# Buffer addresses in a two-layer decoder trunk: a large set that steps by 4096 bytes, and three single tiles

## The chip, the cores and the metric

The kernel runs on one core of one Trainium2 chip. The metric is the device time of one launch in microseconds; the time before is 2398.49 us, the median of three runs (2398.19 to 2398.84). A profile of one execution is there beside the times.

## The reference

A trunk of two layers over 1024 tokens of width 1024, in float32. Layer 0 mixes by an mLSTM with eight heads (key width 64, value width 128) in chunks of 128 tokens. Layer 1 mixes by causal latent attention with eight heads. Each layer ends in an MLP of hidden width 4096 with a squared ReLU, and each norm is modulated by columns computed from the condition `c`.

```python
for l in range(DEPTH):
    sh1, sc1, g1, sh2, sc2, g2 = jnp.split(cond @ ada_w[l] + ada_b[l], 6, axis=-1)
    h = modulate(rmsnorm(x, norm_g[l, 0]), sh1, sc1)
    y = mlstm_mixer(h, ...) if l < N_A else mla_mixer(h, ..., k_nope, k_rope, v, cos, sin)
    x = x + g1[:, None, :] * rmsnorm(y, norm_g[l, 1])
    h = modulate(rmsnorm(x, norm_g[l, 2]), sh2, sc2)
    y = jnp.square(jax.nn.relu(h @ mlp_w1[l])) @ mlp_w2[l]
    x = x + g2[:, None, :] * rmsnorm(y, norm_g[l, 3])
```

In the mLSTM, per chunk: `C_new = decay * C + sum_s w_s k_s v_s^T`, and the output is the sum of a part inside the chunk and a part from the state `C`, divided by a normaliser that is the same sum with ones in place of the values.

## The kernel before, in words

**Split products.** A float32 product is made of three matmuls of the type float32r. An operand is split into a high part and a low remainder (`split_mod` for activations, `wsplit` for weights), and `mm3` (lines 230 to 233) adds low x high (L231), high x low (L232) and high x high (L233) into one PSUM tile. The first operand of a call is the stationary one, which a weight load brings in ahead of the matmul; the second one streams through, up to 512 columns.

**Sets of buffers.** On-chip tiles come from sets, each a tag with a number of buffers that are used in turn: `k4` (24 buffers, "k" in the profile) for split activations, attention keys, values and residual sums; `hd` (8) for hidden blocks and transposed probabilities; `ws` (8; "wh", "wl", and "lw" for weights read back) for split weights; `raw` (4) for weights as they arrive; `tmp`, `tmc`, `tma` for 512-column scratch; `sm1`, `sm4`, `sm8` for a few columns. A set lies in memory where its tag is first used, its buffers one behind the other, and every tile is rounded up to 32 bytes per partition. So the address of a set is the sum of the sizes of what was used before it. A `k4` buffer has 1040 float32 columns (line 120), 4160 bytes; a buffer of `hd`, `ws` or `raw` has 1024, 4096 bytes; one of `tmp`, `tmc` or `tma` has 2048 bytes. The tables of `const` are sets of one buffer.

**The work.** The tokens go in two halves of 512. For each half: norm and modulation, the mLSTM projections (`qk_pairs` or `qk_in`, `gates_in`, `v_in`, `og0`), the parts inside the chunks (`intra0`), the chunks in turn (`chunks0`), the output projection (`wout`), and the MLP (`mlp`). In the MLP, `hidden` makes one block of 128 hidden features: 8 x 3 matmuls with 512 columns, moving tile in k4, stationary tile in ws ("ps<-k,wl" and "ps<-k,wh"). The up-projection multiplies hidden blocks in hd by weights in ws: in the first layer hd moves ("pm<-hd,wh"), in the second hd is stationary and the weights move ("pm<-wh,hd"). From the end of the first MLP on, one half's MLP runs woven with the other half's mixer (`two_streams`, `go`).

**Values.** `v_in` makes the values of a half for four blocks of 128 tokens. Each block has one k4 tile with eight heads of VE = 130 columns: 128 values and two ones, the latter set by a memset on GpSimd (L645), so 8 x 130 = 1040 columns. For each pair of heads j and each block t, 24 matmuls of 256 columns fill a PSUM tile, and one instruction copies it into the block's tile, on ScalarE for even t (L663) and on VectorE for odd t (L661). `chunks0` reads the values per head (L815 for the part inside the chunk, L858 to L860 for the state).

**Gate tables.** `gates0` writes `gc`, the gates by token (L734), and `intra0` writes `dec`, the decay of each chunk (L776). Both come from sets of two buffers, so that each half has its own. Their readers are L758, L825 and L841 for `gc`, and L866 for `dec`.

**What sets the order.** Each engine runs its own queue. A planner orders the instructions by the order of the program, a raised priority for some (`prompt`) and what a buffer's last reader allows; `issue_after` pins the order of some instructions, among them the matmuls of woven streams. A tile that reuses a buffer waits for all readers of the tile before it. The conditioning tables `cond` (L264) and `cols` (L275) are first used behind `raw`, `tmp` and `tma`.

Of the kernel before, what the change touches and what calls it, by code (L numbers as in the profile page):

```python
# [82 lines left out]
def kernel(  # L83
# [33 lines left out]


    def k4(dt=F32):
        t = sb.tile([P, 1040], dt, tag="k4", bufs=K4, name=f"k4_{next(uid)}")  # L120
        return t

    def k4v(dt=F32, b=512):
# [114 lines left out]
    make_identity(nc, ident)  # L238
    ones = const([P, 1], F32, "ones").to_broadcast([P, P])
    dve = nc.vector.memset(ones[:, 0:1], 1.0).ins.engine  # L240
    st1, st2 = raw(), raw()
    L1 = [(norm_g.rearrange("l i (k p) -> (l i k) p", p=P), 64)]
    ab = ada_b.rearrange("l (k p) -> (l k) p", p=P)
# [15 lines left out]
    for st, rows in ((st1, rowsA), (st2, rowsB)):  # L259
        r0 = 0  # L260
        for v, n, w in rows:
            nc.gpsimd.dma_start(st[r0 : r0 + n, :w], v)
            r0 += n
    cond = const([P, KD], F32, "cond")  # L264
    ccol = ps()[:, :8]
    nc.tensor.transpose(ccol, cst[0:8], ident[0:8, 0:8])
    nc.scalar.activation(cond, ccol, AF.Exp, scale=-1.0)
# [3 lines left out]
    condw = tma()[:, :256].rearrange("p (a b) -> p a b", b=32)  # L271
    nc.vector.memset(condw, 0.0)
    nc.vector.tensor_copy(condw[:, :, 0], cond)

    cols = const([P, 200], F32, "cols")  # L275

    def vector_columns():
        for i, st in ((0, st1), (1, st2)):
# [140 lines left out]
    mcol = const([NH, 9], F32, "mcol")  # L419
    nc.vector.memset(mcol, 0.0)  # L420
    Cst = const([P, 4, VE], F32, "Cst")


    def rsqrt_(y, v, t):
# [215 lines left out]
    def v_in(hf):  # L640
        h = hf.h
        hf.v = []
        for t in range(4):
            v = k4().rearrange("p (h e) -> p h e", e=VE)
            nc.gpsimd.memset(v[:, :, 128:VE], 1.0)  # L645
            hf.v.append(v)
        for j in range(4):
            w0 = wload([(0, 0, wcols(w_in, 1024 + j * 256, 256, 0, 4))], 256)
            w1 = wload([(0, 0, wcols(w_in, 1024 + j * 256, 256, 4, 4))], 256)
            for t in range(4):  # L650
                pt = ps()[:, :256]
                for k in range(KD):
                    w = w0 if k < 4 else w1
                    mm3(
                        pt, h.hi[k][:, ts(t, P)], h.lo[k][:, ts(t, P)],
                        w[0][:, k % 4], w[1][:, k % 4], k == 0, k == KD - 1,
                    )
                o = hf.v[t][:, 2 * j : 2 * j + 2, 0:128]
                i = pt.rearrange("p (a b) -> p a b", b=P)
                if t % 2:  # L660
                    nc.vector.tensor_copy(o, i)  # L661
                else:
                    nc.scalar.copy(o, i)  # L663
                yield

    def og0(hf, alloc):
# [11 lines left out]
    def gates0(hf):  # L678

        gp, half = hf.gp, hf.i  # L680
        r8 = lambda: tmc()[0:8]
        t1, t2, t3 = r8(), r8(), r8()
        nc.vector.tensor_copy(t1, gp[64:72])
        nc.vector.scalar_tensor_tensor(t1, gp[0:8], col(GB, 1)[0:8], t1, ALU.add, ALU.add)
        nc.vector.tensor_copy(t2, gp[96:104])
        nc.vector.tensor_copy(t3, gp[32:40])
        nc.vector.scalar_tensor_tensor(t2, t3, col(GB + 1, 1)[0:8], t2, ALU.add, ALU.add)
        ig, fg = t1, t2

        e, u, l = t3, r8(), r8()  # L690
        nc.vector.scalar_tensor_tensor(e, fg, -1.0, fg, ALU.mult, ALU.max)
        nc.scalar.activation(e, e, AF.Exp, scale=-1.0)
        nc.vector.tensor_scalar_add(u, e, 1.0)
        nc.scalar.activation(l, u, AF.Ln)
        nc.vector.scalar_tensor_tensor(e, u, -1.0, e, ALU.add, ALU.subtract)
        nc.vector.scalar_tensor_tensor(l, fg, 0.0, l, ALU.min, ALU.subtract)
        nc.vector.tensor_add(l, l, e)
        b, a, M = t2, t1, t3
        for j in range(4):
            nc.vector.tensor_tensor_scan(  # L700
                b[:, ts(j, P)], ones[0:8], l[:, ts(j, P)], 0.0, ALU.mult, ALU.add
            )
        nc.vector.tensor_sub(a, ig, b)
        for j in range(4):
            g = half * 4 + j
            nc.vector.tensor_tensor_scan(
                M[:, ts(j, P)], ones[0:8], a[:, ts(j, P)], mcol[:, g : g + 1], ALU.mult, ALU.max
            )
            e1 = j * P + P - 1
            nc.vector.tensor_add(mcol[:, g + 1 : g + 2], b[:, e1 : e1 + 1], M[:, e1 : e1 + 1])  # L710
        bc = lambda t: t.unsqueeze(2).to_broadcast([8, 4, P])
        v4 = lambda t: t.rearrange("p (c t) -> p c t", t=P)
        wi, ws_, enm = u, l, b
        nc.vector.tensor_sub(v4(wi), bc(mcol[:, half * 4 : half * 4 + 4]), v4(M))
        nc.scalar.activation(wi, wi, AF.Exp)
        nc.vector.tensor_sub(v4(ws_), v4(a), v4(M)[:, :, P - 1 : P].to_broadcast([8, 4, P]))
        nc.scalar.activation(ws_, ws_, AF.Exp)
        nc.vector.tensor_add(enm, b, M)
        nc.scalar.activation(enm, enm, AF.Exp, scale=-1.0)
        nc.vector.tensor_scalar(RM[0:8], M, -1.0, None, ALU.mult)  # L720
        nc.vector.scalar_tensor_tensor(
            RM[32:40], M, -1.0, RM[0:8].bitcast(F32), ALU.mult, ALU.subtract
        )
        wh = tmc(F32R)[0:8]
        nc.vector.tensor_copy(wh, wi)
        nc.vector.tensor_copy(RM[64:72], wh.bitcast(F32))
        nc.vector.tensor_sub(RM[96:104], wi, wh.bitcast(F32))
        yield
        pt = pc()[:, :96].rearrange("p (c r) -> p c r", r=24)
        for j in range(4):  # L730
            for i, rows in enumerate((a, ws_, enm)):
                nc.tensor.transpose(pt[:, j, ts(i, 8)], rows[:, ts(j, P)], ident[0:8, 0:8])
        hf.gc = const_rot("gc", [P, 4, 24])
        nc.vector.tensor_copy(hf.gc, pt)  # L734
        yield

    def const_rot(tag, shape, n=2):
        return sb.tile(shape, F32, tag=tag, bufs=n, name=f"{tag}_{next(uid)}")

    def intra0(hf):  # L740

        hf.PT = []
        hf.dec = const_rot("dec", [P, 4, 4])
        for p_ in range(4):
            qp, kp = hf.q[p_ // 2][:, p_ % 2], hf.k[p_ // 2][:, p_ % 2]
            PT = hdv()
            E = [tmc(), tmc()]
            for r in range(2):
                hh = 2 * p_ + r
                pt = pc()  # L750
                nc.tensor.matmul(
                    pt, maskA, identb.unsqueeze(1).to_broadcast([P, 4, P]), start=True, stop=False
                )
                nc.tensor.matmul(
                    pt, e8[:, hh : hh + 1].to_broadcast([P, P]), RM, start=False, stop=True
                )
                for j in range(4):
                    nc.scalar.activation(  # L758
                        E[r][:, ts(j, P)], pt[:, ts(j, P)], AF.Exp,
                        bias=hf.gc[:, j, hh : hh + 1],  # L760
                    )
                yield
            st = pm()
            for j in range(4):
                for r in range(2):
                    nc.tensor.matmul(
                        st[:, r, ts(j, P)], kp[ts(r, 64), ts(j, P)], qp[ts(r, 64), ts(j, P)],
                        start=True, stop=True,
                    )
            for r in range(2):  # L770
                nc.vector.tensor_mul(PT[:, r], st[:, r], E[r])
                yield
            pt = pc()
            nc.tensor.matmul(pt, selW[:, p_], RM, start=True, stop=True)
            nc.vector.tensor_mul(qp, qp, pt)
            nc.vector.tensor_copy(hf.dec[:, p_], pt.rearrange("p (c t) -> p c t", t=P)[:, :, P - 1])  # L776
            hf.PT.append(PT)
            yield
# [14 lines left out]
    def chunks0(hf):  # L793
# [4 lines left out]
        for j in range(4):  # L798
# [4 lines left out]
            for q in range(2):  # L803
                num = pm()
                nv = num[:, :, 0 : 2 * VE].rearrange("p b (i e) -> p b i e", e=VE)
                for i in range(2):
                    p_ = 2 * q + i

                    for r in range(2 if g > 0 else 0):
                        nc.tensor.matmul(  # L810
                            nv[:, r, i], hf.q[p_ // 2][ts(r, 64), p_ % 2, cs],
                            Cst[ts(r, 64), p_], start=True, stop=False,
                        )
                    for r in range(2):
                        nc.tensor.matmul(  # L815
                            nv[:, r, i], hf.PT[p_][:, r, cs], v[:, 2 * p_ + r],
                            start=g == 0, stop=True,
                        )
                nvs.append(nv)
# [33 lines left out]
            for b2 in range(2 if g < 7 else 0):  # L853
                uv = pc()[:, 0 : 2 * VE].rearrange("p (i e) -> p i e", e=VE)
                for i in range(2):
                    for r in range(2):
                        hh = 2 * (2 * b2 + i) + r
                        nc.tensor.matmul(  # L858
                            uv[ts(r, 64), i], kw[:, ts(hh, 64)], v[:, hh], start=True, stop=True
                        )  # L860
                for i in range(2):
                    p_, u = 2 * b2 + i, uv[:, i]
# [1100 lines left out]
```

## Time and profile before

| | |
|---|---|
| time, median of three runs | 2398.49 us |
| span of the profiled execution | 2395.7 us |
| its own time: span and what lies around it | the median less the span is 2.8 us |
| TensorE matmul busy (99%) | 2364.8 us, 11621 instructions |
| TensorE weight load busy (81%) | 1945.5 us |
| VectorE busy (65%) | 1550.3 us |
| ScalarE busy (44%) | 1054.9 us |
| GpSimd busy (1%) | 18.3 us |
| DMA, mean | 156 GB/s |
| granted TensorE clock | 0.997 |

The page names a group of instructions by its line, engine and operation, by the tile written and the tiles read (for a matmul the moving one first), by shape and count; then come its busy time in us and the mean of one in ns, and the time its engine sat idle before it with what ended that idle time. The records of two matmuls that follow each other overlap, so the mean of one is longer than the step from one start to the next; the timeline gives the starts.

### The profile page before, as it was taken

What the parts mean: (1) busy time and instruction counts of PE and PEld (TensorE: products, weight loads), DVE (VectorE), ACT (ScalarE), POOL (GpSimd) and SP (SyncE); (2) the same over time, 40 slices, a digit from 0 to 9 for tenths busy, and PEclk for the clock granted to TensorE, in tenths of its full rate; (3) what the DMA queues carried; (4) which work ended last, traced back from release to release, by engine and by line L of the source; (5) the groups of instructions that cost most, each with busy time, mean ns of one, the idle gap of its engine ahead of it and who ended that gap; (6) DMA issues with size and microseconds to landing.
All of it is one profiled execution on the core that took longest, in us unless ns stands there. A gap on an engine that the chain in (4) does not pass through costs nothing.

```text
span 2395.7 us, 30518 instructions
## 1 busy us (share of the span) xinstructions
PE 2364.8 (99%) x11621; PEld 1945.5 (81%) x11621; DVE 1550.3 (65%) x2431; ACT 1054.9 (44%) x1712; POOL 18.3 (1%) x91
## 2 busy tenths in 40 slices
PE   7999999999999999999999999999999999999998
PEld 5888888788888887888888877888888888888886
DVE  6667866858656677877764867766566386353345
ACT  4355334655333454444444554344444353443333
POOL 1000000000000000000000000000000000000000
PEclk9999999999999999999999999999999999999999
DMA  8442654544654745545543444864424354354431
GB/s 310 148 143 81 192 178 134 165 132 150 189 171 152 243 138 179 159 160 186 168 137 114 153 162 153 260 240 133 139 97 150 105 167 128 101 189 140 144 99 62
DMA packets 377106, 374.48 MB, mean 156 GB/s; under 512 B 24355, under 2 KB 282464, under 8 KB 376960
## 3 DMA queue, kind: packets, MB, share of 16 engines
q1 hardware_dynamic: 376672, 372.44, 48.9%
q8 instruction: 91, 1.49, 0.3%
q14 instruction: 55, 0.45, 0.1%
q0 software_dynamic: 288, 0.10, 0.0%
HBM read 313.24 MB, written 59.24 MB: 155 GB/s over the span
## 4 chain that ended last, share of the span: by engine, by line
PE 91%; DVE 4%; DMA 3%; ACT 1%; issue 1%; SPq 0%; DVEq 0%; ACTq 0%
PE ps L231 17%; PE ps L232 17%; PE ps L233 17%; PE pm L231 10%; PE pm L232 10%; PE pm L233 10%; PE pc L1445 1%; PE pc L231 1%; PE pc L233 1%; PE pc L232 1%; PE pm L815 1%; PE pm L1331 1%; DMA raw<-in_mlp_w_dram 1%; DVE wl L190 1%; PE pm L1325 1%
## 5 line engine op out<-in xcount | busy, mean ns | idle before, releaser
L190 DVE TENSOR_TENSOR wl<-raw,wh 128x1024 fp32r<-128x1024 f32 (+2 forms) x366 | 438.7, 1202 | 449.5 <-ACT wh L189 442.3
L189 ACT CAST wh<-raw 128x1024 fp32r<-128x1024 f32 (+2 forms) x366 | 376.0, 1032 | 717.0 <-PE ps L231 392.2
L231 PE MATMUL ps<-k,wl 128*128 128x512 f32 x1528 | 611.0, 400 | 2.3 <-ACT k L671 1.4
L233 PE MATMUL ps<-k,wh 128*128 128x512 f32 x1528 | 601.0, 393 | 0.0
L232 PE MATMUL ps<-k,wh 128*128 128x512 f32 x1528 | 600.9, 393 | 0.0
L231 PEld LDWEIGHTS ps<-k,wl 128*128 128x128 f32 x1528 | 287.0, 188 | 69.7 <-issue 2.9
L233 PEld LDWEIGHTS ps<-k,wh 128*128 128x128 f32 x1528 | 287.0, 188 | 67.3 <-issue 0.5
L232 PEld LDWEIGHTS ps<-k,wh 128*128 128x128 f32 x1528 | 287.5, 188 | 63.6 <-issue 1.7
L198 DVE TENSOR_TENSOR k<-k,pm 128x512 f32<-128x512 f32 (+1 forms) x254 | 210.9, 859 | 107.0 <-PE pm L233 106.5
L231 PE MATMUL pm<-hd,wl 128*128 128x512 f32 x512 | 202.0, 394 | 0.4 <-ACT hd L470 0.4
L233 PE MATMUL pm<-hd,wh 128*128 128x512 f32 x512 | 199.8, 391 | 0.0
L232 PE MATMUL pm<-hd,wh 128*128 128x512 f32 x512 | 199.5, 390 | 0.2 <-DVE hd L471 0.2
L231 PE MATMUL pm<-wh,hd 128*128 128x512 f32 x488 | 192.9, 395 | 3.2 <-ACT raw L1337 2.9
L232 PE MATMUL pm<-wl,hd 128*128 128x512 f32 x488 | 191.3, 392 | 0.0
L233 PE MATMUL pm<-wh,hd 128*128 128x512 f32 x488 | 190.3, 390 | 0.0
L360 DVE SCALAR_TENSOR_TENSOR tma<-raw,cond,tma 128x512 f32<-128x512 f32 x168 | 125.6, 747 | 20.6 <-DMA raw<-in_kv_ada_w_dram 14.6
L471 DVE TENSOR_TENSOR hd<-tmp,hd 128x512 fp32r<-128x512 f32 x128 | 88.3, 690 | 56.8 <-ACT hd L470 56.5
L1337 ACT ACTIVATE raw<-pm,sm 128x128 f32<-128x128 f32 (+3 forms) x64 | 47.5, 742 | 151.3 <-DVE sm L1336 122.7
L232 PEld LDWEIGHTS pm<-hd,wh 128*128 128x128 f32 x512 | 96.2, 188 | 21.3 <-DVE hd L471 0.5
L231 PEld LDWEIGHTS pm<-hd,wl 128*128 128x128 f32 x512 | 96.1, 188 | 21.2 <-ACT hd L470 0.8
L233 PEld LDWEIGHTS pm<-hd,wh 128*128 128x128 f32 x512 | 96.1, 188 | 21.1
L231 PEld LDWEIGHTS pm<-wh,hd 128*128 128x128 f32 x488 | 91.6, 188 | 24.9 <-ACT raw L1337 5.5
(347 smaller groups left out, 3414.5 us busy)
## 6 DMA issues: line engine op xcount, KB each, us to landing
raw<-in_mlp_w_dram SPq DMA_DIRECT2D x256, 512.0 KB, 4.1
raw<-in_ada_w_dram SPq DMA_DIRECT2D x80, 512.0 KB, 4.3
raw<-in_a_w_in_dram SPq DMA_DIRECT2D x48, 512.0 KB, 4.1
xs<-k SPq DMA_DIRECT2D x40, 256.0 KB, 4.8
raw<-in_kv_ada_w_dram SPq DMA_DIRECT2D x16, 512.0 KB, 3.8
raw<-in_a_w_out_dram SPq DMA_DIRECT2D x16, 512.0 KB, 4.6
kd<-k SPq DMA_DIRECT2D x32, 256.0 KB, 3.7
vd<-k SPq DMA_DIRECT2D x32, 256.0 KB, 5.0
```

The lines of the kernel that those rows point to most:

```text
L189: nc.scalar.copy(hi[:, :n], r[:, :n])
L190: i = nc.vector.tensor_sub(lo[:, :n], r[:, :n], hi[:, :n].bitcast(F32))
L198: return f(*a, **k)
L231: nc.tensor.matmul(o, ll, rh, start=start, stop=False)
L232: nc.tensor.matmul(o, lh, rl, start=False, stop=False)
L233: pe_last[0] = nc.tensor.matmul(o, lh, rh, start=False, stop=stop)
L360: nc.vector.scalar_tensor_tensor(acc, r[:, kk], cond[:, k : k + 1], acc, ALU.mult, ALU.add)
L471: nc.vector.tensor_sub(lo, u, hi.bitcast(F32))
L815: nc.tensor.matmul(nv[:, r, i], hf.PT[p_][:, r, cs], v[:, 2 * p_ + r], start=g == 0, stop=True,)
L1325: nc.tensor.matmul(o[:, :w], ql, kh, start=True, stop=False)
L1331: nc.tensor.matmul(o[:, :w], qh, kh, start=False, stop=True)
L1337: nc.scalar.activation(pr[:, :n], f, AF.Exp, bias=m, scale=SCALE, accum_out=l)
```

## The change

The k4 buffer has 1024 columns in place of 1040. The values of a block are now in two places: heads 0 to 6 in the block's k4 tile (7 x 130 = 910 columns), head 7 of all four blocks in a new tile `last` of 4 x 130 columns in a set `v8` with one buffer. The ones of `last` are set by a memset of their own. For the last pair of heads (j = 3) the copy out of PSUM is made in two pieces of 128 columns. `gc` and `dec` become single tables that both halves use. `cond` and `cols` are made ahead of `raw`, and `gc` and `dec` behind `Cst`, so that their sizes come at other places in the sum of addresses. What is computed stays the same.

```diff
     def k4(dt=F32):
-        t = sb.tile([P, 1040], dt, tag="k4", bufs=K4, name=f"k4_{next(uid)}")
+        t = sb.tile([P, 1024], dt, tag="k4", bufs=K4, name=f"k4_{next(uid)}")
...
     dve = nc.vector.memset(ones[:, 0:1], 1.0).ins.engine
+    cond = const([P, KD], F32, "cond")
+    cols = const([P, 200], F32, "cols")
     st1, st2 = raw(), raw()
...
-    cond = const([P, KD], F32, "cond")
...
-    cols = const([P, 200], F32, "cols")
...
     Cst = const([P, 4, VE], F32, "Cst")
+    gc = const([P, 4, 24], F32, "gc")
+    dec = const([P, 4, 4], F32, "dec")
...
+        last = sb.tile([P, 4, VE], F32, tag="v8", bufs=1, name=f"v8_{next(uid)}")
+        nc.gpsimd.memset(last[:, :, 128:VE], 1.0)
         for t in range(4):
-            v = k4().rearrange("p (h e) -> p h e", e=VE)
+            v = k4()[:, : 7 * VE].rearrange("p (h e) -> p h e", e=VE)
             nc.gpsimd.memset(v[:, :, 128:VE], 1.0)
-            hf.v.append(v)
+            hf.v.append([v[:, h_] for h_ in range(7)] + [last[:, t]])
+            hf.v[t].append(v)
...
-                o = hf.v[t][:, 2 * j : 2 * j + 2, 0:128]
                 i = pt.rearrange("p (a b) -> p a b", b=P)
-                if t % 2:
-                    nc.vector.tensor_copy(o, i)
+                if j < 3:
+                    parts = [(hf.v[t][8][:, 2 * j : 2 * j + 2, 0:128], i)]
                 else:
-                    nc.scalar.copy(o, i)
+                    parts = [(hf.v[t][6 + e][:, 0:128], i[:, e]) for e in range(2)]
+                for o, a in parts:
+                    if t % 2:
+                        nc.vector.tensor_copy(o, a)
+                    else:
+                        nc.scalar.copy(o, a)
...
-        hf.gc = const_rot("gc", [P, 4, 24])
+        hf.gc = gc
...
-    def const_rot(tag, shape, n=2):
-        return sb.tile(shape, F32, tag=tag, bufs=n, name=f"{tag}_{next(uid)}")
-
...
-        hf.dec = const_rot("dec", [P, 4, 4])
+        hf.dec = dec
...
-                            nv[:, r, i], hf.PT[p_][:, r, cs], v[:, 2 * p_ + r],
+                            nv[:, r, i], hf.PT[p_][:, r, cs], v[2 * p_ + r],
...
-                            uv[ts(r, 64), i], kw[:, ts(hh, 64)], v[:, hh], start=True, stop=True
+                            uv[ts(r, 64), i], kw[:, ts(hh, 64)], v[hh], start=True, stop=True
```

## The prediction

> **What bounds the kernel now.** I read the page first: its head, the busy times and the chain of waits.
>
> ```profile
> span 2395.7 us, 30518 instructions
> PE 2364.8 (99%) x11621; PEld 1945.5 (81%) x11621; DVE 1550.3 (65%) x2431; ACT 1054.9 (44%) x1712; POOL 18.3 (1%) x91
> PEclk9999999999999999999999999999999999999999
> ```
>
> PE is busy for 99% of the span at full granted clock, and the next engine, DVE, for 65%. So the time is the sum of the steps from one matmul's start to the next, and hardly anything else. That busy time cannot say whether those steps are as short as they could be. Next came the groups by line with shapes kept apart: the matmuls with 512 moving columns, which are most of the program.
>
> ```profile
> L231 PE MATMUL ps<-k,wl 128*128 128x512 f32 x1528 | 611.0, 400 | 2.3 <-ACT k L671 1.4 <-DVE wl L190 0.8
> L233 PE MATMUL ps<-k,wh 128*128 128x512 f32 x1528 | 601.0, 393 | 0.0
> L232 PE MATMUL ps<-k,wh 128*128 128x512 f32 x1528 | 600.9, 393 | 0.0
> ...
> L231 PE MATMUL pm<-hd,wl 128*128 128x512 f32 x512 | 202.0, 394 | 0.4 <-ACT hd L470 0.4
> L233 PE MATMUL pm<-hd,wh 128*128 128x512 f32 x512 | 199.8, 391 | 0.0
> L232 PE MATMUL pm<-hd,wh 128*128 128x512 f32 x512 | 199.5, 390 | 0.2 <-DVE hd L471 0.2
> L231 PE MATMUL pm<-wh,hd 128*128 128x512 f32 x488 | 192.9, 395 | 3.2 <-ACT raw L1337 2.9
> L232 PE MATMUL pm<-wl,hd 128*128 128x512 f32 x488 | 191.3, 392 | 0.0
> L233 PE MATMUL pm<-wh,hd 128*128 128x512 f32 x488 | 190.3, 390 | 0.0
> ```
>
> After the arrow stands the moving operand, then the stationary one. All nine rows are one operation of one shape, with next to no waits (2.3 us before 1528 of them). Yet with the moving operand in the large set (k) all three lines average (611.0 + 601.0 + 600.9) / 4584 = 395.5 ns; between hd and the weight set (wl, wh) they average (202.0 + 199.8 + 199.5) / 1536 = 391.3 and (192.9 + 191.3 + 190.3) / 1464 = 392.4 ns. A record overlaps its successor, so I turned to the timeline of TensorE for the true step.
>
> ```profile
> 1237.04 0.40 PE L231 MATMUL pm<-hd,wl 128*128 128x512 f32 x1
> ...
> 1242.50 0.40 PE L231 MATMUL ps<-k,wl 128*128 128x512 f32 x1
> ...
> 1287.14 0.40 PE L231 MATMUL ps<-k,wl 128*128 128x512 f32 x1
> ...
> 1292.70 0.39 PE L231 MATMUL pm<-hd,wl 128*128 128x512 f32 x1
> ...
> 1298.17 0.40 PE L231 MATMUL ps<-k,wl 128*128 128x512 f32 x1
> ```
>
> From 1237.04 to 1242.50 stand 24 matmuls with hd: 5.46 / 24 = 227.5 ns a step. From 1242.50 to 1287.14 stand 192 (eight hidden blocks of 24) with k: 44.64 / 192 = 232.5 ns. From 1292.70 to 1298.17 stand 24 with hd again: 227.9 ns. Over that k stretch the grouped view gives a mean record of 395 ns:
>
> ```profile
> L231 PE MATMUL ps<-k,wl 128*128 128x512 f32 x64 | 25.3, 395 | 0.0
> ```
>
> So a record is some 162 ns longer than its step, for k (395 - 232.5) as for hd (390 to 391 less 227.5 to 227.9), and a difference of records is a difference of steps. PE loses 3 to 5 ns on each matmul that touches the large set.
>
> Is it the k set, or the pair of sets? The other 512-column groups answer.
>
> ```profile
> L1327 PE MATMUL pm<-hd,k 128*128 128x512 f32 x48 | 19.0, 396 | 0.4 <-DMA k<-td 0.4
> L1328 PE MATMUL pm<-hd,k 128*128 128x512 f32 x48 | 19.0, 395 | 0.0
> L1326 PE MATMUL pm<-k,k 128*128 128x512 f32 x48 | 18.9, 394 | 0.0
> L232 PE MATMUL ps<-k,lw 128*128 128x512 f32 x80 | 31.4, 394 | 0.0
> L233 PE MATMUL ps<-k,lw 128*128 128x512 f32 x80 | 31.2, 393 | 0.0
> L232 PE MATMUL pm<-k,wh 128*128 128x512 f32 x64 | 25.6, 400 | 0.0
> L233 PE MATMUL pm<-k,wh 128*128 128x512 f32 x64 | 25.3, 395 | 0.0
> L232 PE MATMUL pc<-k,wh 128*128 128x512 f32 x48 | 19.0, 396 | 0.0
> L233 PE MATMUL pc<-k,wh 128*128 128x512 f32 x48 | 18.9, 394 | 0.0
> ```
>
> hd is fast beside wh, and slow (395 to 396) when the stationary tile is k. k is slow in all three PSUM sets, so PSUM is not the cause. What hd and wh share and k does not is the step of their buffers: 1024 x 4 = 4096 bytes = 8 x 512, against 1040 x 4 = 4160 = 8 x 512 + 64. The eight ws and eight hd buffers lie one behind the other, all at one offset modulo 512; the 24 k4 buffers run through all eight multiples of 64. My reading: the stationary read of the next matmul runs beside the moving read of this one, and the step depends on the distance of their addresses; a distance that is a multiple of 512 bytes gives the short step.
>
> **The change, part by part.**
>
> *Addresses.* k4 steps by 4096. cond and cols move ahead of raw. Between k4 and the next set now lie, each rounded up to 32 bytes, ada 384, kvada 64, mods 288, identb 256, maskA 256, e8 32, selW 2048, RM 2048, mcol 64, Cst 2080, gc 384, dec 64, lbias 32 and six small tiles 192: 8192 = 16 x 512 in all. So raw, tmp, tma, k4, tmc, ws and hd all have one offset, and every pair with k gets the relation that hd and ws have already (their own is unchanged). The matmuls it reaches: 3 x 1528 = 4584 in the k rows above, 3 x 64 (pm<-k), 3 x 48 (pc<-k), 3 x 80 and 3 x 16 with raw and lw, 5 x 48 in the scores: 5448. For the gain of each there are four differences: all lines 395.5 - 391.3 = 4.2 and 395.5 - 392.4 = 3.1; L232 and L233 alone, which hold no waits, 393.3 - 389.9 = 3.4 and 393.3 - 391.0 = 2.3. I take **3.3 ns**: 5448 x 3.3 = **18.0 us**. Bounds: 2.3 gives 12.5 us; the clean stretch, 232.5 - 227.5 = 5.0, gives 27 us. A price of nothing or below stands with the rivals.
>
> The Trainium skill speaks against this. Its page "TensorE: Matmul & The Clock Gate", section "Step-by-step: what each phase is for", says that loading the next weights takes no read bandwidth from the running matmul, and "SBUF — State Buffer", section "Who interferes with whom", says "PE and ACT never wait on anyone". By these the sum of this part would be zero; the rows above, 395.5 against 391.3 ns for one shape, do not fit them.
>
> *256-column matmuls.*
>
> ```profile
> L232 PE MATMUL ps<-wl,k 128*128 128x256 f32 x288 | 80.8, 281 | 0.0
> L1328 PE MATMUL pm<-hd,k 128*128 128x256 f32 x32 | 9.0, 280 | 0.0
> ```
>
> With other partners they take the same 280 to 281 ns, and no aligned pair of this shape is there to compare. I take nothing; some 1600 of them at 1 ns either way would be 1.6 us.
>
> *Eight more copies.* The last pair of heads (j = 3) is copied out as two 128-column pieces for each of the four token blocks of a half, two by ACT and two by DVE: four copies more a half, eight in all.
>
> ```profile
> L663 ACT COPY k<-ps x16: 352/373/397, 87.7 to 325.5; 128x256 f32<-128x256 f32 x16
> L661 DVE COPY k<-ps x16: 408/418/426, 91.6 to 329.9; 128x256 f32<-128x256 f32 x16
> L202 ACT COPY k<-ps 128x512 f32<-128x512 f32 x24 | 13.9, 579 | 6.8 <-PE ps L233 6.8
> L734 DVE COPY gc<-pc x1: 258/258/258, 252.3 to 252.3; 128x96 f32<-128x96 f32 x1
> ```
>
> ACT: (579 - 373) / 256 = 0.8 ns a column, so 128 columns take 373 - 103 = 270 and the pair 540, 167 more than now. DVE: (418 - 258) / 160 = 1.0, so 290 and 580, 162 more. For the eight blocks of both halves that is 8 x 0.165 = 1.3 us on two engines. A block's 24 matmuls, at 281 - 162 = 119 ns a step, take 2.9 us, and two ps buffers turn, so the 0.58 us hides under the next block: nothing on PE. Uncovered it would be the 1.3 us. The two memsets more fall on POOL, 1% busy.
>
> *Single tiles.* gc, dec and the last head's tile lose their second buffer, so half 1 must wait until half 0 has read them.
>
> ```profile
> L841 DVE TENSOR_TENSOR sm<-sm,gc x8: 152/152/154, 150.6 to 211.7; 128x4 f32<-128x4 f32 x8
> L866 DVE SCALAR_TENSOR_TENSOR Cst<-Cst,dec,pc x12: 340/342/350, 175.4 to 214.0; 128x130 f32<-128x130 f32 x12
> L776 DVE COPY dec<-pc x4: 153/154/155, 263.9 to 327.9; 128x4 f32<-128x4 f32 x4
> L815 PE MATMUL pm<-k,hd x64: 272/275/378, 126.5 to 205.2; 128*128 128x130 f32 x64
> L645 POOL MEMSET k<- x4: 113/115/116, 216.6 to 218.2; 128x16 f32 x4
> ```
>
> Half 0 reads gc until 211.7 and half 1 writes it at 252.3: 40 us to spare. dec: 214.0 and 263.9, 50 us. The last head's tile is read by L815 until 205.2 and by the state update, whose sums end at 214.0; its memset comes at 216.6 and its copies nearly 100 us later. Behind it in POOL's queue wait the four value memsets, needed at the copies from 280 us on. No wait on the path: 0. The cover goes only if the planner moves half 1's gates up by over 40 us.
>
> **Sum.** The profiled execution: 2395.7 - 18.0 = 2377.7 us of span. The runs' median of 2398.49 lies 2.8 us above that span, for what lies around it: 2380.5 us timed. Nothing absorbs the gain, since PE waits for almost nothing in these groups.
>
> **The rivals.**
> - *No change, 2398.5 us.* The step belongs to the form of the accumulation, not to addresses; the skill's two sentences say the same. For it: hidden blocks and up-projections are different loops. Against: hd is slow beside k and fast beside wh. It would need all these pairs to differ in something else.
> - *Partial gain, 2389.5 us.* The hd tile holds its high and low halves 2048 bytes apart, the large set holds them in two tiles; or the place within 512 matters as well as the distance, and only half the pairs get the short step: 9 us. For it: the nine rows differ among themselves (390 to 395) although all are aligned. Against: wh and wl are separate tiles too, and are as fast when they move.
> - *Slower, 2435 us.* At one offset, moving and stationary read start in the same place and collide on each matmul. Price: the slowest row without waits, L232 pm<-k,wh at 400 ns, for all: (400 - 393.3) x 5448 = 36.5 us. It decides from the point at which ps<-k in L232 and L233 averages over 393.3. Against: 3000 matmuls run aligned now, at 390 to 395.
>
> **How the numbers follow.** Forecast, 2375 to 2388: 0.72. Partial, to 2392: 0.14. No change: 0.08. Slower: 0.06. A measurement here tells 0.2%, 4.8 us, from no change. Faster is then 0.72 + 0.14 = 0.86, same 0.08, slower 0.06. The range of 2374 to 2392 holds the forecast and most of the partial gain.
>
> **What would show it.** In the changed kernel's groups, ps<-k in L232 and L233 should have 390 to 391 ns for 393, L1327 and L1328 should fall from 395 to some 391, and the hd rows should stay. Eight hidden blocks in a row should take 43.7 us for 44.6. The 256-column rows stay at 280. No wait for gc, dec or the last head's tile should stand among PE's releasers. If ps<-k keeps 393, the address is not the cause; if hd with wh moves too, the place within 512 matters and not the distance alone.

## The result, and the profile after

The changed kernel takes 2378.23 us (median of four runs, 2377.37 to 2379.25), the kernel before 2398.34 us (four runs, 2397.82 to 2398.84): a ratio of 0.9914, with a 95% interval of 0.990 to 0.9928. That is 20.1 us less; the forecast was 18.0 us less, 2380.5 us.

The head of the page after, and its chain of waits by engine:

```profile
span 2375.5 us, 30534 instructions
PE 2343.4 (99%) x11621; PEld 1946.7 (82%) x11621; DVE 1549.6 (65%) x2435; ACT 1055.6 (44%) x1716; POOL 18.2 (1%) x93
...
PEclk9999999999999999999999999999999999999999
...
PE 89%; DVE 4%; DMA 4%; ACT 1%; issue 1%; SPq 0%; DVEq 0%; ACTq 0%
```

The span fell by 20.2 us (from 2395.7) and the busy time of TensorE by 21.4 us (from 2364.8), with the same 11621 matmuls at the same granted clock. TensorE is still busy for 99%: nothing took its place as the bound, and each matmul simply takes less. Which ones, the groups with shapes kept apart tell (after):

```profile
L231 PE MATMUL ps<-k,wl 128*128 128x512 f32 x1528 | 605.2, 396 | 2.5 <-ACT k L679 1.4 <-DVE wl L190 0.9 <-DVE tmc L694 0.2
L233 PE MATMUL ps<-k,wh 128*128 128x512 f32 x1528 | 596.1, 390 | 0.0
L232 PE MATMUL ps<-k,wh 128*128 128x512 f32 x1528 | 595.6, 390 | 0.0
L231 PE MATMUL pm<-hd,wl 128*128 128x512 f32 x512 | 200.9, 392 | 0.5 <-ACT hd L471 0.5
L232 PE MATMUL pm<-hd,wh 128*128 128x512 f32 x512 | 199.3, 390 | 0.2 <-DVE hd L472 0.2
L233 PE MATMUL pm<-hd,wh 128*128 128x512 f32 x512 | 199.2, 389 | 0.0
...
L231 PE MATMUL ps<-wh,k 128*128 128x256 f32 x288 | 82.7, 288 | 1.8 <-ACT v L671 1.1 <-DVE k L669 0.7
L232 PE MATMUL ps<-wl,k 128*128 128x256 f32 x288 | 81.4, 283 | 0.0
...
L232 PE MATMUL pm<-k,wh 128*128 128x512 f32 x64 | 25.2, 394 | 0.0
L1332 PE MATMUL pm<-hd,k 128*128 128x512 f32 x48 | 18.9, 393 | 0.5 <-DMA k<-td 0.5
L1333 PE MATMUL pm<-hd,k 128*128 128x512 f32 x48 | 18.8, 392 | 0.0
```

The k rows of L232 and L233 went from 393 to 390 ns, so they now stand where hd with the weights stands; all three lines went from 395.5 to (605.2 + 596.1 + 595.6) / 4584 = 392.0 ns. The scores (L1327 and L1328 before, L1332 and L1333 now) went from 396 and 395 to 393 and 392. The 256-column rows went the other way, from 281 to 283.

The timeline of TensorE shows the steps themselves:

```profile
1229.88 0.40 PE L231 MATMUL pm<-hd,wl 128*128 128x512 f32 x1
...
1235.35 0.39 PE L231 MATMUL ps<-k,wl 128*128 128x512 f32 x1
...
1284.31 0.39 PE L231 MATMUL pm<-hd,wl 128*128 128x512 f32 x1
...
1289.75 0.39 PE L231 MATMUL ps<-k,wl 128*128 128x512 f32 x1
```

24 matmuls with hd take 5.47 us (227.9 ns a step) and, later, 5.44 us (226.7 ns). Between them stand 216 with k, nine hidden blocks in a row: 48.96 / 216 = 226.7 ns. Before, the same kind of stretch had 232.5 ns.

To see all of it, I summed the busy times of the matmul groups in three classes: 512 columns with a tile of the k4 set on either side (5480 matmuls), 512 columns between hd and the weights (3072), and 256 columns (1600). The ns are the sum over the count. The last column is the ratio to the kernel before, with its interval. The six rows below the first two are experiments of the next part.

| kernel | large set, 512 col. | hd and weights, 512 col. | 256 col. | ratio |
|---|---|---|---|---|
| before | 2170.3 us, 396.0 ns | 1203.7 us, 391.8 ns | 454.9 us, 284.3 ns | 1 |
| after | 2151.5 us, 392.6 ns | 1200.6 us, 390.8 ns | 457.4 us, 285.9 ns | 0.9914 (0.990 to 0.9928) |
| k_tables | 2171.6 us, 396.3 ns | 1202.8 us, 391.5 ns | 454.8 us, 284.2 ns | 1.0010 (1.0001 to 1.0019) |
| k_all192 | 2153.2 us, 392.9 ns | 1200.3 us, 390.7 ns | 458.1 us, 286.3 ns | 0.9929 (0.991 to 0.9949) |
| k_dist256 | 2152.6 us, 392.8 ns | 1200.7 us, 390.9 ns | 457.2 us, 285.8 ns | 0.9922 (0.9908 to 0.9937) |
| k_dist64 | 2163.1 us, 394.7 ns | 1203.9 us, 391.9 ns | 453.7 us, 283.6 ns | 0.9959 (0.9944 to 0.9974) |
| k_dist128 | 2177.1 us, 397.3 ns | 1202.7 us, 391.5 ns | 457.1 us, 285.7 ns | 1.0027 (1.0018 to 1.0037) |
| k_dist192 | 2177.3 us, 397.3 ns | 1202.5 us, 391.4 ns | 452.7 us, 282.9 ns | 1.0028 (1.0017 to 1.0039) |

From before to after: -18.8, -3.1 and +2.5 us, together -19.4 of the 20.2 us by which the span fell. Records overlap, so these sums are only near to the time itself; the starts, which give the steps, come with the experiments.

### The profile page after: what moved, and what is told of

Read it like the earlier page. It is cut to its first block, busy times and chain, and to the rows that moved or that the text cites. A ratio compares the mean times of both kernels' runs of the same rounds, so it can differ in the third digit from the quotient of the medians.

```text
span 2375.5 us, 30534 instructions
## 1 busy us (share of the span) xinstructions
PE 2343.4 (99%) x11621; PEld 1946.7 (82%) x11621; DVE 1549.6 (65%) x2435; ACT 1055.6 (44%) x1716; POOL 18.2 (1%) x93
## 4 chain that ended last, share of the span: by engine, by line
PE 89%; DVE 4%; DMA 4%; ACT 1%; issue 1%; SPq 0%; DVEq 0%; ACTq 0%
PE ps L231 16%; PE ps L233 16%; PE ps L232 16%; PE pm L231 9%; PE pm L232 9%; PE pm L233 9%; PE pc L1450 1%; DMA raw<-in_a_w_in_dram 1%; DMA raw<-in_mlp_w_dram 1%; PE pc L231 1%; PE pc L233 1%; PE pc L232 1%; PE pm L1336 1%; DVE wl L190 1%; PE pm L820 1%
## 5 line engine op out<-in xcount | busy, mean ns | idle before, releaser
L231 PE MATMUL ps<-k,wl 128*128 128x512 f32 x1528 | 605.2, 396 | 2.5 <-ACT k L679 1.4
L233 PE MATMUL ps<-k,wh 128*128 128x512 f32 x1528 | 596.1, 390 | 0.0
L232 PE MATMUL ps<-k,wh 128*128 128x512 f32 x1528 | 595.6, 390 | 0.0
L231 PEld LDWEIGHTS ps<-k,wl 128*128 128x128 f32 x1528 | 287.0, 188 | 65.1 <-issue 2.9
L233 PEld LDWEIGHTS ps<-k,wh 128*128 128x128 f32 x1528 | 286.8, 188 | 61.7 <-issue 0.5
L232 PEld LDWEIGHTS ps<-k,wh 128*128 128x128 f32 x1528 | 287.2, 188 | 58.8 <-issue 1.7
L231 PE MATMUL pm<-hd,wl 128*128 128x512 f32 x512 | 200.9, 392 | 0.5 <-ACT hd L471 0.5
L232 PE MATMUL pm<-hd,wh 128*128 128x512 f32 x512 | 199.3, 390 | 0.2 <-DVE hd L472 0.2
L233 PE MATMUL pm<-hd,wh 128*128 128x512 f32 x512 | 199.2, 389 | 0.0
L231 PE MATMUL pm<-wh,hd 128*128 128x512 f32 x488 | 192.2, 394 | 1.6 <-ACT raw L1342 1.3
L232 PE MATMUL pm<-wl,hd 128*128 128x512 f32 x488 | 190.9, 391 | 0.0
L233 PE MATMUL pm<-wh,hd 128*128 128x512 f32 x488 | 190.2, 390 | 0.0
L231 PEld LDWEIGHTS pm<-hd,wl 128*128 128x128 f32 x512 | 96.2, 188 | 20.8 <-ACT hd L471 0.9
L232 PEld LDWEIGHTS pm<-hd,wh 128*128 128x128 f32 x512 | 96.1, 188 | 20.5 <-DVE hd L472 0.5
L233 PEld LDWEIGHTS pm<-hd,wh 128*128 128x128 f32 x512 | 96.1, 188 | 20.2
L231 PEld LDWEIGHTS pm<-wh,hd 128*128 128x128 f32 x488 | 91.6, 188 | 22.3 <-ACT raw L1342 3.5
```

The costliest lines, as they stand in the source:

```text
L231: nc.tensor.matmul(o, ll, rh, start=start, stop=False)
L232: nc.tensor.matmul(o, lh, rl, start=False, stop=False)
L233: pe_last[0] = nc.tensor.matmul(o, lh, rh, start=False, stop=stop)
```

## The experiments

The prediction's theory was: the distance between the moving and the stationary tile sets the step, and a multiple of 512 bytes is short. Against it stood that the place within 512 bytes counts and not the distance; that it is enough if all buffers of the large set have one offset among themselves, whatever the other sets have; that the gain comes from the small edits (the single tables, the tables moved ahead); and that the short distances have a period other than 512. The kernels k_dist64 to k_dist256 and k_all192 differ from the changed kernel by the lines shown; the addresses of the sets are moved by moving a table, and nothing else is touched.

**The small edits alone.** The changed kernel with the k4 buffer of 1040 columns and the values as before, so that single tables (`gc`, `dec`) and the tables ahead of raw (`cond`, `cols`) are what is left of the change.

```
-        t = sb.tile([P, 1024], dt, tag="k4", bufs=K4, name=f"k4_{next(uid)}")
+        t = sb.tile([P, 1040], dt, tag="k4", bufs=K4, name=f"k4_{next(uid)}")
...
-            v = k4()[:, : 7 * VE].rearrange("p (h e) -> p h e", e=VE)
+            v = k4().rearrange("p (h e) -> p h e", e=VE)
...
-                            nv[:, r, i], hf.PT[p_][:, r, cs], v[2 * p_ + r],
+                            nv[:, r, i], hf.PT[p_][:, r, cs], v[:, 2 * p_ + r],
```

> The kernel before with only the small edits: gc and dec single, cond and cols made ahead of raw. k4 keeps its step of 4160 bytes, so it stays scattered; raw, tmc, ws and hd share one offset. Theory 1: the k rows stay at 393 ns in L232 and L233, 2396-2400 us, no wait for gc or dec on TensorE. Rival (the single tables or the new order of the small tables bring the gain): 2378 us. The hd rows, 1 ns shorter after the change, tell apart whether that came from the new place of the sets (they fall here too) or from their neighbours in the k set (they stay at 390-391).

Measured: 2401.24 us against 2398.46, a ratio of 1.0010 (1.0001 to 1.0019), a little above the 2396 to 2400 us expected. The groups with shapes kept apart, k_tables:

```profile
L232 PE MATMUL ps<-k,wh 128*128 128x512 f32 x1528 | 601.3, 394 | 0.0
L233 PE MATMUL ps<-k,wh 128*128 128x512 f32 x1528 | 601.1, 393 | 0.0
```

The small edits bring no gain, and the k rows keep the 393 to 394 ns of before. All of the gain needs the k4 step of 4096 bytes.

**The distance by 64 bytes.** A table of 64 bytes moves from behind the large set to ahead of raw: raw, tmp, tma and k4 are then 64 bytes off the places of tmc, ws and hd.

```
     cols = const([P, 200], F32, "cols")
+    kvada = const([P, 16], F32, "kvada")
     st1, st2 = raw(), raw()
...
     ada = const([P, 2, 48], F32, "ada")
-    kvada = const([P, 16], F32, "kvada")
```

> The changed kernel with the table kvada (64 bytes) made ahead of the raw set, so that raw, tmp, tma and all 24 k4 buffers lie 64 bytes further along modulo 512 than tmc, ws and hd. The k4 buffers still step by 4096 and still share one offset among themselves. Theory 1 (the distance between the moving and the next stationary read, modulo 512, sets the step): ps<-k in L232 and L233 goes back from 390 to 392-394 ns, hd with wh stays at 389-390, the time goes back to 2390-2400 us. Rival (it is enough that the k4 buffers share one offset among themselves): ps<-k stays at 390, 2378 us.

Measured: 2388.21 us, ratio 0.9959 (0.9944 to 0.9974). The groups, k_dist64:

```profile
L233 PE MATMUL ps<-k,wh 128*128 128x512 f32 x1528 | 600.2, 393 | 0.0
L232 PE MATMUL ps<-k,wh 128*128 128x512 f32 x1528 | 596.9, 391 | 0.0
```

About half of the gain is gone, with every buffer of the large set still at one offset. A common offset alone doesn't give the full gain. The loss is smaller than was expected: 2388.21 us lies below the 2390 to 2400 us.

**The distance by 256 bytes.** The same with a table of 256 bytes (`identb`).

> The changed kernel with the table identb (256 bytes) made ahead of the raw set: k4 and raw lie 256 bytes away from ws and hd modulo 512. Theory 1 (distance): ps<-k in L232 and L233 at 392-394 ns for 390, 2390-2400 us, if 256 is as bad a distance as the mean of the scattered ones was. Rival (one offset inside the large set is enough): 390 ns, 2378 us.

Measured: 2379.65 us, ratio 0.9922 (0.9908 to 0.9937). The groups, k_dist256:

```profile
L233 PE MATMUL ps<-k,wh 128*128 128x512 f32 x1528 | 596.3, 390 | 0.0
L232 PE MATMUL ps<-k,wh 128*128 128x512 f32 x1528 | 595.8, 390 | 0.0
```

Nearly as fast as the change, with intervals that overlap, where the theory had expected 2390 to 2400 us. So 512 falls as the period: 256 bytes off is as good as none. By itself this run would also suit the rival that one offset inside the large set is enough; k_dist64, and the next two distances, speak against that one.

**All sets moved together by 192 bytes.** Six tiles of eight columns are made ahead of raw, by one added line.

```
     cols = const([P, 200], F32, "cols")
+    nc.vector.memset(small(8), 0.0)
     st1, st2 = raw(), raw()
```

> The changed kernel with the set of six 8-column tiles (192 bytes) made first, so that all sets move by 192 bytes together: every distance between sets stays as in the changed kernel, the place within 512 goes from 480 to 160. Theory 1 (distance alone): 2378 us, within 0.2%, ps<-k 390 ns. Rival (the place within 512 bytes counts): ps<-k and hd with wh both move by 1 ns or more, 5 us or more.

Measured: 2380.95 us, ratio 0.9929 (0.991 to 0.9949). The groups, k_all192:

```profile
L233 PE MATMUL ps<-k,wh 128*128 128x512 f32 x1528 | 596.5, 390 | 0.0
L232 PE MATMUL ps<-k,wh 128*128 128x512 f32 x1528 | 595.1, 389 | 0.0
```

All sets are 192 bytes further on, and the rows stay: here the distance counts and not the place.

**The distance by 384 and 448 bytes (128 and 192 modulo 256).** `gc` (384 bytes) moves ahead of raw, then `gc` and `kvada` (448). If one offset within the large set were enough, both would still be faster than before.

```
     cols = const([P, 200], F32, "cols")
+    gc = const([P, 4, 24], F32, "gc")          # both kernels
+    kvada = const([P, 16], F32, "kvada")       # the second one only
     st1, st2 = raw(), raw()
```

> The changed kernel with gc (384 bytes) made ahead of raw: raw, tmp, tma and k4 lie 128 bytes from ws and hd modulo 256; the k4 buffers share one offset among themselves as in the changed kernel. Theory 2 (distance modulo 256 bytes, with the steps that the scan gave): k moving over ws at some 232.4 ns a step for 227.5, 5112 matmuls, +25 us; 256-column rows 118.7 for 119.6, -1 us: 2402 us, slower than the kernel before. Rival (one offset inside the large set is enough): 2378 us.

> The same with gc and kvada (448 bytes) ahead of raw: a distance of 192 bytes modulo 256. Theory 2: 233.3 ns a step for 227.5, 5112 matmuls, +29.6 us; the 256-column matmuls, whose distance has the other sign (64), 117.8 for 119.6, -2.7 us: 2405 us. Rival (one offset is enough): 2378 us.

Measured: 2405.36 us, ratio 1.0027 (1.0018 to 1.0037), and 2406.06 us, ratio 1.0028 (1.0017 to 1.0039). The groups, first k_dist128:

```profile
L233 PE MATMUL ps<-k,wh 128*128 128x512 f32 x1528 | 603.7, 395 | 0.0
L232 PE MATMUL ps<-k,wh 128*128 128x512 f32 x1528 | 603.2, 395 | 0.0
```

and k_dist192:

```profile
L233 PE MATMUL ps<-k,wh 128*128 128x512 f32 x1528 | 603.5, 395 | 0.0
L232 PE MATMUL ps<-k,wh 128*128 128x512 f32 x1528 | 603.5, 395 | 0.0
```

Both are slower than the kernel before, whose buffers are scattered over all offsets, and 27 to 28 us slower than the change, from 384 or 448 bytes of tables that lie elsewhere. They hold every other part of the change, so neither the single tables nor the split values can be what made it faster. The kernel before mixes the four distances: the mean of the four aligned kernels' large-set records, (392.6 + 394.7 + 397.3 + 397.3) / 4 = 395.5 ns, is near its 396.0.

**The step by itself.** A small kernel of its own runs blocks of 60 equal matmuls of the type float32r, one behind the other, with the other engines idle. Each block moves the moving tile by 64 bytes against the stationary one; then the same with 256 columns, with both tiles moved alike, and with finer offsets.

```
def block(kind, i, m0, s0, n):
    o = pp.tile([P, 512], F32, tag="ps", bufs=2, name=name(kind, i))
    for j in range(60):
        nc.tensor.matmul(o[:, :n], st[:, s0 : s0 + P], mv[:, m0 : m0 + n], start=j == 0, stop=j == 59)
for i in range(33): block("wide", i, 16 * i, 0, 512)
for i in range(33): block("half", i, 16 * i, 0, 256)
for i in range(9): block("both", i, 16 * i, 16 * i, 512)
for i, c in enumerate((2, 4, 8, 12, 20, 24)): block("fine", i, c, 0, 512)
```

> A kernel of its own, which computes nothing of the reference: blocks of 60 float32r matmuls with one moving tile and one stationary tile, every other engine idle. From block to block the moving tile shifts by 64 bytes (33 blocks, with 512 and with 256 columns), then both tiles shift alike (9 blocks), then the moving tile by 8 to 96 bytes. Theory 1 (distance): with 512 columns the step is shortest, some 227 ns (record 390), where the shift is a multiple of 512 bytes, and 3 to 5 ns longer between; shifting both alike changes nothing. Rival (the lost time needs the other engines' reads and writes beside it): one step for all shifts. With 256 columns theory 1 gives no number; the changed kernel's 256-column rows, 2 ns longer than before, would need multiples of 512 to be a bad distance there.

The timeline of TensorE, scan1. Each row is one block; the step is the difference of two starts over 60.

```profile
57.24 13.91 PE L33 MATMUL wideab<-mv,st 128*128 128x512 f32 x60
70.99 14.11 PE L33 MATMUL wideac<-mv,st 128*128 128x512 f32 x60
84.94 14.16 PE L33 MATMUL widead<-mv,st 128*128 128x512 f32 x60
98.94 13.78 PE L33 MATMUL wideae<-mv,st 128*128 128x512 f32 x60
112.56 13.91 PE L33 MATMUL wideaf<-mv,st 128*128 128x512 f32 x60
...
499.80 7.36 PE L33 MATMUL halfaa<-mv,st 128*128 128x256 f32 x60
506.99 7.23 PE L33 MATMUL halfab<-mv,st 128*128 128x256 f32 x60
514.06 7.28 PE L33 MATMUL halfac<-mv,st 128*128 128x256 f32 x60
521.17 6.96 PE L33 MATMUL halfad<-mv,st 128*128 128x256 f32 x60
527.98 7.34 PE L33 MATMUL halfae<-mv,st 128*128 128x256 f32 x60
...
732.32 13.79 PE L33 MATMUL bothaa<-mv,st 128*128 128x512 f32 x60
745.95 13.80 PE L33 MATMUL bothab<-mv,st 128*128 128x512 f32 x60
```

With 512 columns a distance of 64 bytes takes 13.75 / 60 = 229.2 ns a step, 128 bytes 232.5, 192 bytes 233.3 and 256 bytes 227.0, and this repeats every 256 bytes to the end of the scan. With 256 columns the distances 0, 64, 128 and 192 take 119.8, 117.8, 118.5 and 113.5 ns: another order, in which 0 is the worst. With both tiles moved alike the step stays at 227 ns. Distances that are no multiple of 64 (8, 16, 32, 48, 80 and 96 bytes) take 231 to 234 ns. No other engine works here and nothing but the moving tile's address differs between the blocks, so the loss needs no other engine: it lies within what TensorE itself reads.

The kernels have the same steps. From the starts in their traces, the mean step from a matmul of ps<-k,wl or ps<-k,wh with 512 columns to the next matmul (some 4490 of the 4584, steps of 300 ns and more left out) is 227.5 ns after, 229.5 in k_dist64, 232.8 in k_dist128, 227.6 in k_dist256 and 233.3 in k_dist192, for 227.0, 229.2, 232.5, 227.0 and 233.3 in the scan. Before it was 231.3, near the mean of the four distances, 230.5.

**Whose stationary tile, which width, which type.** A second small kernel lets two pairs of tiles take turns. In "own" each matmul has a distance of 0 to its own stationary tile and c to the one that follows; in "next" it is the other way round (c is 128, 192 and 64 bytes). Then the number of columns changes, and last the type (bf16).

```
for i, c in enumerate((32, 48, 16)):            # columns of 4 bytes
    pair("own", i, (0, c), (0, c))              # offsets of moving, stationary
    pair("next", i, (0, c), (c, 0))
for n in (128, 192, 256, 320, 384, 448, 512):   # four distances each
    for i in range(4): block(f"n{LET[n // 64]}", i, 16 * i, 0, n)
for n in (256, 512):                            # bf16, four distances each
    ...
```

> A kernel of its own, which computes nothing of the reference, all other engines idle. First pairs of moving and stationary tiles that alternate, so that a matmul's own distance is 0 and that to the next stationary tile is c, or the reverse (c = 128, 192, 64 bytes). Theory 2a (the read for the next weight load runs beside this matmul's moving read): the blocks with the next distance 0 take 226.7 ns a step, those with the own distance 0 take 231 to 233. Theory 2b (the own pair counts): the reverse. Then 128 to 512 moving columns at distances 0, 64, 128, 192: if the loss is one of whole 64-byte pieces, steps are 0.417 ns a column plus a multiple of 6.67 ns that depends on the distance. Then bf16 tiles with 256 and 512 columns at the same four distances in bytes: if the loss hangs on the 4-byte reads alone, they are equal.

The timeline of TensorE, scan2:

```profile
43.19 13.88 PE L48 MATMUL ownaa<-mv,st 128*128 128x512 f32 x60
56.91 13.96 PE L48 MATMUL nextaa<-mv,st 128*128 128x512 f32 x60
70.71 14.07 PE L48 MATMUL ownab<-mv,st 128*128 128x512 f32 x60
84.61 14.16 PE L48 MATMUL nextab<-mv,st 128*128 128x512 f32 x60
98.61 14.06 PE L48 MATMUL ownac<-mv,st 128*128 128x512 f32 x60
...
415.51 13.11 PE L69 MATMUL bfiaa<-mbf,sbf 128*128 128x512 bf16 x60
428.46 13.11 PE L69 MATMUL bfiab<-mbf,sbf 128*128 128x512 bf16 x60
441.41 13.11 PE L69 MATMUL bfiac<-mbf,sbf 128*128 128x512 bf16 x60
454.36 13.11 PE L69 MATMUL bfiad<-mbf,sbf 128*128 128x512 bf16 x60
```

With c = 128 "own" takes 13.72 / 60 = 228.7 ns and "next" 230.0; with c = 192 they take 231.7 and 233.3. With c = 64 they take the same as with 192: the sign of the distance turns from one matmul to the next, so that in both cases 64 and 192 modulo 256 alternate. Neither kind reaches the 227.0 of a pure distance of 0, and where only the next stationary tile is at distance 0 the step is the longer one. So the prediction's reading, that the stationary read of the next matmul alone meets this one's moving read, isn't borne out, and neither is its opposite. The two distances don't simply share the loss either: with half of them at 0, 231.7 ns still lies above the 231.25 that the pure blocks at 64 and 192 bytes give on average. In these blocks the tiles also jump by c from one matmul to the next, which no block tries by itself. How the two reads meet within a step stays open.

bf16 takes 12.95 / 60 = 215.8 ns at all four distances, and with 256 columns 109.2. So the loss hangs on the type: bf16 has none of it. The Trainium skill's page "TensorE: Matmul & The Clock Gate", section "Step-by-step: what each phase is for", gives 512 / 2.4 + 2.5 = 216 ns for a step of 512 columns. bf16 agrees, with 215.8, while float32r takes 227.0 ns at its best distance and 233.3 at its worst.

By columns, from the same timeline: with 128, 192 and 320 columns all four distances are alike within 1 ns (111 to 112 ns for the first two, 146 to 147 for 320); with 384 they take 173 to 177, with 448 200 to 204, with 512 227 to 233 ns. The expectation of steps in whole multiples of 6.67 ns doesn't fit all widths.

## Why the prediction was right, point by point

**The main term holds, in size too.** The prediction's 5448 matmuls at 3.3 ns, 18.0 us, stand against 18.8 us over the 5480 of the table, 3.4 ns each; the four steps of scan1 give 230.5 - 227.0 = 3.5 ns for a mix of all distances. What carried it was the comparison of rows of one shape with other partners; the clean stretch of the timeline (5.0 ns then, 232.5 - 226.7 = 5.8 ns now) would have been too much for the mean, since the large set had all distances, 0 too. "A difference of records is a difference of steps" holds only roughly: by the starts, the step of ps<-k fell by 231.3 - 227.5 = 3.8 ns, its record by 395.5 - 392.0 = 3.5. Of the signs, eight hidden blocks take 192 x 226.7 ns = 43.5 us for the 43.7 forecast, and the score rows (L1332 and L1333 now) stopped at 393 and 392 for some 391.

**The period was wrong, without harm.** "A distance that is a multiple of 512 bytes" is a multiple of 256 (k_dist256, scan1). Before, the only aligned sets stepped by 4096 bytes, so that the trace could not tell 512 from 256; the change aligned to 512, which is a multiple of 256 too.

**"The next matmul's stationary read" isn't borne out** (scan2), though the rule drawn from it, equal offsets, gives the short step. With equal offsets the own and the next distance are both 0, so the change could not tell the two apart; that the reading was wrong cost nothing here, which is luck.

**"The hd rows should stay"** is wrong by 3.1 us: 391.8 to 390.8 ns, 3072 times. By the prediction's own sign this would mean that the place counts; k_all192 says that it doesn't. In k_tables, k_dist64, k_dist128 and k_dist192 hd and the weights have the distances of the change among themselves, and these rows keep 391.4 to 391.9 ns; they fall to 390.7 to 390.9 only where the large set is aligned as well (after, k_all192, k_dist256). So this gain comes only together with that of the large set's matmuls, between which they run. How a neighbour would pass it on wasn't settled.

**"256-column matmuls: nothing"** is wrong by 2.5 us the other way, 284.3 to 285.9 ns. Its bound of 1 ns on each of 1600 was too narrow. scan1 gives the cause: with this width a distance of 0 takes 119.8 ns and the other three 113.5 to 118.5. The steps of ps<-wl,k agree for 0 (120.0 after), 128 (118.9 in k_dist128) and 64 bytes (117.4 in k_dist192); here k is stationary, so its distance has the other sign. They don't for 192 (k_dist64): 116.7 on average for 113.5, with a third of them at 113 and 114 and the others longer. The two terms that were put at nothing, -3.1 and +2.5, nearly cancelled, which is luck as well.

**The eight copies** take what was estimated one by one, and less in pairs. From the answer on the last head's tile (v), kernel after; the three times are least, median and most in ns; the last two rows tell who waited for it, with the us in all and how often:

```profile
L671 ACT COPY v<-ps x4: 266/269/272, 139.7 to 326.4; 128x128 f32<-128x128 f32 x4
L669 DVE COPY v<-ps x4: 281/281/283, 140.5 to 330.2; 128x128 f32<-128x128 f32 x4
L645 POOL MEMSET v<- x2: 106/116/125, 6.6 to 212.2; 128x8 f32 x2
...
  POOL v L645: 56.2, 1
...
  PE ps L231: 1.1, 1
```

269 ns on ScalarE for the estimate of 270, and 281 on VectorE for 290. The two copies of a pair overlap, though, as the timeline of ScalarE, kernel after, shows:

```profile
319.40 0.27 ACT L671 COPY k<-ps 128x128 f32<-128x128 f32 x1 [1.50 <-PE ps L233]
319.56 0.27 ACT L671 COPY v<-ps 128x128 f32<-128x128 f32 x1
```

The pair is done 0.43 us after its start, where the prediction had 0.54. "Hidden under the next block" holds but for one wait of 1.1 us, the 1.1 at L231 ps<-wh,k in the groups above. That the second piece caused it isn't shown: k_tables, which copies each pair of heads in one piece, waits 0.8 and 0.5 us for copies at the same row.

**The single tiles** cost no wait of TensorE: neither gc nor dec stands among its releasers after, and k_tables shows no gain or loss beyond 0.1 to 0.2%. The second memset of v waits 56.2 us on GpSimd for the state update of the first half and starts at 212.2, over 100 us ahead of the second half's first copy into that tile (319.56): nothing waits for it.

**The rivals.** "No change" fell: one operation of one shape takes 227.0 to 233.3 ns by its addresses alone, with no other engine at work. Of the two sentences of the Trainium skill that the prediction set against the gain, the one in "SBUF — State Buffer", section "Who interferes with whom", "PE and ACT never wait on anyone", is about other engines. scan1, where none works, neither confirms nor contradicts it. The prediction's other one, on the weight load, fits the four equal steps of bf16, and not those of float32r with 512 columns. "Partial gain" fell: the k rows took all of the short step, 390 ns, and the place didn't count in k_all192 and scan1. "Slower, the reads collide at one offset" fell for 512 columns, where 0 is the best distance; its direction is right for 256 columns, where 0 is the worst, and a common offset of the wrong size does make the kernel slower than none (2405.36 and 2406.06 us).

No run was faster than the change. The 256-column matmuls would want another offset between the same tiles than the 512-column ones: k_dist64 gave most of them the distance of 192 that is best in scan1, and their class fell by 3.7 us against the change (457.4 to 453.7), while the large set's rose by 11.6.

## What to carry to other kernels

Where an engine is busy for 99% and its rows of one shape have different mean times, group them by the tiles they read, and compare the addresses of those tiles: the layout can be the cause. For float32r matmuls with 512 moving columns, as they ran here, give the moving and the stationary sets the same offset modulo 256 bytes, and check it again after every small table that is added ahead of a set, since 64 bytes more cost half of the gain and 128 or 192 more than all of it. Before such an edit is trusted, a loop of 60 equal matmuls for each distance shows the price of every width and type by itself.

## What the runs showed of the hardware that I had not expected

- The step of a float32r matmul with 512 columns depends on the distance of its two tiles modulo 256 bytes: 227.0, 229.2, 232.5 and 233.3 ns at 0, 64, 128 and 192 bytes; bf16 takes 215.8 ns at each.
- The order is another one with 256 columns: 119.8, 117.8, 118.5 and 113.5 ns. With 128, 192 and 320 columns the four distances lie within 1 ns.
- With 128 and with 192 columns of float32r the step is the same, 111 to 112 ns.
- A table of 384 bytes in another place made the whole kernel 27 us slower than the change (2405.36 against 2378.23 us), with the same 30534 instructions.
